# Rotating 96 images on one core: loads of 16 rows to a partition in place of 8

## The chip, the cores and the metric

One NeuronCore of one Trainium2 chip runs the kernel. The metric is device time in microseconds (us), the median of several runs. All runs quoted here are fast, that is, none was over 1.5% above the fastest of its kernel. The profile's span is some 1.8 us shorter than the device time, because it starts at the first instruction.

The traffic is 25.17 MB in and 25.17 MB out. "MB" of a slab or a buffer means 2^20 bytes; the profile's MB and GB/s are decimal. The profile also keeps a record of every packet (queue, start, duration, bytes); "by the records" below means that the bytes of each packet are spread over its duration, while the views count a packet whole where it starts.

## The reference

```python
def setup_inputs():
    batch, c, h, w = 32, 3, 256, 256
    return {"x": np.random.randn(batch, c, h, w).astype(np.float32)}

def reference(x):
    return np.rot90(x, k=-1, axes=(-2, -1)).astype(np.float32)
```

Each of the 96 images of 256 x 256 floats is rotated by 90 degrees clockwise: row h of the input becomes column 255 - h of the output.

## The kernel before

A slab is 1 MB, four images. Each partition gets 8 consecutive rows of an image (8 KB). VectorE transposes blocks of 32 partitions by 32 elements, after which each partition holds 8 consecutive output rows, and the slab is stored. Loads are issued from SyncE (SP in the profile), stores from ScalarE (ACT).

```python
    R = 8
    G = H // R
    n_slabs = B * C * G // P          # 24
    SHORT = 2
    ld_v = x.rearrange("b c h w -> (b c h) w").rearrange("(n p r) w -> n p (r w)", p=P, r=R)
    st_v = out.rearrange("b c h w -> (b c h) w").rearrange("(n p c) w -> n p (c w)", p=P, c=R)
    in_pool = ctx.enter_context(tc.tile_pool(name="in_pool", bufs=12))
    out_pool = ctx.enter_context(tc.tile_pool(name="out_pool", bufs=12))

    for n in range(n_slabs):
        t_in = in_pool.tile([P, R * W], fp32, tag="t_in")
        nc.sync.dma_start(out=t_in, in_=ld_v[n])
        t_out = out_pool.tile([P, R * W], fp32, tag="t_out")
        src = t_in.rearrange("p (r g c) -> p c r g", r=R, c=R)
        dst = t_out.rearrange("p (c g r) -> p c r g", c=R, r=R)[:, :, ::-1, ::-1]
        parts = 2 if n in (0, n_slabs - 1) else 1
        for k in range(parts):
            cs = slice(k * R // parts, (k + 1) * R // parts)
            nc.vector.transpose(out=dst[:, cs], in_=src[:, cs])
        nc.scalar.dma_start(out=st_v[n], in_=t_out,
                            max_dma_last_dim=2048 if n < SHORT else 8192)
    # (launch code cut)
```

`max_dma_last_dim` sets the size in bytes of one packet: the first two slabs are stored in 2 KB packets, the rest in 8 KB packets.

Of the kernel before, what the change touches and what calls it, by code (L numbers as in the profile page):

```python
# [1 line left out]

# [4 lines left out]


@with_exitstack  # L10
def kernel(
    ctx: ExitStack,
    tc: tile.TileContext,
    x: bass.AP,
    out: bass.AP,
):










    nc = tc.nc
    fp32 = mybir.dt.float32

    B, C, H, W = x.shape  # L30
    P = nc.NUM_PARTITIONS
    R = 8
    G = H // R
    n_slabs = B * C * G // P
    SHORT = 2

    ld_v = x.rearrange("b c h w -> (b c h) w").rearrange("(n p r) w -> n p (r w)", p=P, r=R)
    st_v = out.rearrange("b c h w -> (b c h) w").rearrange("(n p c) w -> n p (c w)", p=P, c=R)

    in_pool = ctx.enter_context(tc.tile_pool(name="in_pool", bufs=12))  # L40
    out_pool = ctx.enter_context(tc.tile_pool(name="out_pool", bufs=12))

    for n in range(n_slabs):
        t_in = in_pool.tile([P, R * W], fp32, tag="t_in")
        nc.sync.dma_start(out=t_in, in_=ld_v[n])  # L45

        t_out = out_pool.tile([P, R * W], fp32, tag="t_out")
        src = t_in.rearrange("p (r g c) -> p c r g", r=R, c=R)
        dst = t_out.rearrange("p (c g r) -> p c r g", c=R, r=R)[:, :, ::-1, ::-1]
        parts = 2 if n in (0, n_slabs - 1) else 1  # L50
        for k in range(parts):
            cs = slice(k * R // parts, (k + 1) * R // parts)
            nc.vector.transpose(out=dst[:, cs], in_=src[:, cs])  # L53

        nc.scalar.dma_start(out=st_v[n], in_=t_out,
                            max_dma_last_dim=2048 if n < SHORT else 8192)


# [1 line left out]
_INS = ['x']  # L60
_OUTS = [((32, 3, 256, 256), 'float32')]


# [23 lines left out]
```

## Time and profile before

| | before |
|---|---|
| device time, median of 3 (range) | 124.11 us (124.02 to 124.44) |
| span of the profile | 122.4 us |
| DMA: mean rate; plateau | 411 GB/s; about 428 GB/s |
| load queue, store queue: time of their packets | 49.1% and 49.0% of 16 engines' span |
| VectorE (DVE) busy | 91.6 us (75%) |

The page of the kernel before. The DVE and DMA rows show busy tenths in 40 equal slices of the span (9 is 90% or more), the GB/s row what moved in each slice; q1 is the load queue and q10 the store queue, with packets, MB and the time of their packets as a share of 16 engines' span.

```profile
span 122.4 us, 164 instructions
...
DVE  0199999999999999999999999697796793000000
...
DMA  2999999999999999999999999999999999999994
GB/s 83 426 428 428 390 428 424 422 421 426 424 428 418 428 426 420 426 428 428 426 428 428 428 428 428 428 426 426 428 428 428 426 428 428 428 428 426 428 428 193
...
q1 hardware_dynamic: 3456, 25.17, 49.1%
q10 hardware_dynamic: 4224, 25.17, 49.0%
```

The reader is to see that the DMA row is 9 in every slice but the first and the last, while VectorE stops being busy some 20 us before the end. Time can only be won by moving the same bytes at a higher rate, or by shortening the two ends. The one weak slice inside, 390 GB/s, is where the first stores join the loads.

### The profile page before, as it was taken

Reading aid. Unit: us, or ns where it says so; the run is one execution under the profiler, and the core shown is the slowest. Engines: PE = TensorE matmul, PEld = TensorE weight load, DVE = VectorE, ACT = ScalarE, POOL = GpSimd, SP = SyncE. Lnnn points to the kernel's source line nnn. Section 1 sums busy time; section 2 is a strip of 40 time slices with the busy share of each in tenths; the row PEclk is TensorE's granted clock in tenths of the full one; section 3 lists DMA queues with packets and bytes.
Section 4 is the critical chain, followed back from the end, with each engine's and each line's share of the span. In section 5 each row is a group of like instructions: output and inputs, shape, how many; then the busy total and the mean of one; then the engine's idle time right before and its main releaser. Section 6 shows DMA issues by size and latency. Waiting matters only on the chain.

```text
span 122.4 us, 164 instructions
## 1 busy us (share of the span) xinstructions
DVE 91.6 (75%) x26; POOL 0.2 (0%) x4
## 2 busy tenths in 40 slices
DVE  0199999999999999999999999697796793000000
POOL 0000000000000000000000000000000000000000
DMA  2999999999999999999999999999999999999994
GB/s 83 426 428 428 390 428 424 422 421 426 424 428 418 428 426 420 426 428 428 426 428 428 428 428 428 428 426 426 428 428 428 426 428 428 428 428 426 428 428 193
DMA packets 7680, 50.33 MB, mean 411 GB/s; under 512 B 768, under 2 KB 768, under 8 KB 1792
## 3 DMA queue, kind: packets, MB, share of 16 engines
q1 hardware_dynamic: 3456, 25.17, 49.1%
q10 hardware_dynamic: 4224, 25.17, 49.0%
HBM read 25.17 MB, written 25.17 MB: 411 GB/s over the span
## 4 chain that ended last, share of the span: by engine, by line
DMA 78%; DVE 2%; DVEq 2%; SPq 1%; issue 0%
DMA t_in<-in_x_dram 78%; DVE t_out L53 2%; DVEq L82 2%; SPq L45 1%; DVEq L53 0%
## 5 line engine op out<-in xcount | busy, mean ns | idle before, releaser
L53 DVE STREAM_TRANSPOSE t_out<-t_in 128x2048 f32<-128x2048 f32 (+1 forms) x26 | 91.6, 3647 | 10.4 <-DMA t_in<-in_x_dram 10.4
L71 POOL MEMSET const-bfloat16-1.0<- 128x1 bf16 x1 | 0.1, 102 | 0.0
L71 POOL MEMSET const-uint8-127<- 128x1 uint8 x1 | 0.1, 102 | 0.0
L71 POOL MEMSET const-float32-0.0<- 128x1 f32 x1 | 0.1, 99 | 0.2 <-issue 0.2
L71 POOL MEMSET const-float32-1.0<- 128x1 f32 x1 | 0.1, 99 | 0.0
## 6 DMA issues: line engine op xcount, KB each, us to landing
t_in<-in_x_dram SPq DMA_DIRECT2D x24, 1024.0 KB, 14.4
out_dram<-t_out ACTq DMA_DIRECT2D x24, 1024.0 KB, 19.5
```

The lines of the kernel that those rows point to most:

```text
L45: nc.sync.dma_start(out=t_in, in_=ld_v[n])
L53: nc.vector.transpose(out=dst[:, cs], in_=src[:, cs])
L71: nc = _bacc.Bacc("TRN2", target_bir_lowering=False, num_devices=1)
L82: with _tile.TileContext(nc) as tc:
```

## The change

Its intent: larger DMA packets. A slab becomes 2 MB (eight images); each partition gets 16 rows (16 KB) of one image. So that a block of 32 partitions still transposes into whole output partitions, the two halves of a slab are interleaved: two loads of 64 partitions each, one to the even and one to the odd partitions. The first slab keeps the old layout, so that work starts as soon as before, and is stored in 2 KB packets. Buffers halve in number and keep their bytes.

```diff
-    R = 8
-    SHORT = 2
+    RI, RO = 16, 8
+    K = H // RI
+    I = 2
+    Q = P // (K * I)
+    n_slabs = B * C // (Q * I)        # 12
...
-    in_pool = ctx.enter_context(tc.tile_pool(name="in_pool", bufs=12))
-    out_pool = ctx.enter_context(tc.tile_pool(name="out_pool", bufs=12))
+    in_pool = ctx.enter_context(tc.tile_pool(name="in_pool", bufs=6))
+    out_pool = ctx.enter_context(tc.tile_pool(name="out_pool", bufs=6))
     for n in range(n_slabs):
...
+        if n == 0:
+            for i in range(I):
+                nc.sync.dma_start(out=t_in[:, i], in_=ld8_v[n, i])
+                (transpose of half i, as before)
+        else:
+            t_flat = t_in.rearrange("p i f -> p (i f)")
+            for i in range(I):
+                nc.sync.dma_start(out=t_flat[i::I], in_=ld16_v[n, i])
+            src = t_flat.rearrange("p (r g c) -> p c r g", r=RI, c=RO)
+            dst = t_out.rearrange("p i (c k r) -> p c r k i", c=RO, r=RI)[:, :, ::-1, ::-1, :]
+            for h in range(2):
+                cs = slice(h * RO // 2, (h + 1) * RO // 2)
+                nc.vector.transpose(out=dst[:, cs], in_=src[:, cs])
+        for i in range(I):
+            nc.scalar.dma_start(out=st_v[n, i], in_=t_out[:, i],
+                                max_dma_last_dim=2048 if n == 0 else 8192)
```

More of the change, by code (lines that the diff above doesn't have):

```diff
@@ L31 @@
     P = nc.NUM_PARTITIONS
-    R = 8
-    G = H // R
-    n_slabs = B * C * G // P
-    SHORT = 2
-    ld_v = x.rearrange("b c h w -> (b c h) w").rearrange("(n p r) w -> n p (r w)", p=P, r=R)
-    st_v = out.rearrange("b c h w -> (b c h) w").rearrange("(n p c) w -> n p (c w)", p=P, c=R)
-    in_pool = ctx.enter_context(tc.tile_pool(name="in_pool", bufs=12))
-    out_pool = ctx.enter_context(tc.tile_pool(name="out_pool", bufs=12))
-    for n in range(n_slabs):
-        t_in = in_pool.tile([P, R * W], fp32, tag="t_in")
-        nc.sync.dma_start(out=t_in, in_=ld_v[n])
-        t_out = out_pool.tile([P, R * W], fp32, tag="t_out")
-        src = t_in.rearrange("p (r g c) -> p c r g", r=R, c=R)
-        dst = t_out.rearrange("p (c g r) -> p c r g", c=R, r=R)[:, :, ::-1, ::-1]
-        parts = 2 if n in (0, n_slabs - 1) else 1
-        for k in range(parts):
-            cs = slice(k * R // parts, (k + 1) * R // parts)
-            nc.vector.transpose(out=dst[:, cs], in_=src[:, cs])
-        nc.scalar.dma_start(out=st_v[n], in_=t_out,
-                            max_dma_last_dim=2048 if n < SHORT else 8192)
+    RI, RO = 16, 8
@@ new lines @@
+    K = H // RI
+    I = 2
+    Q = P // (K * I)
+    n_slabs = B * C // (Q * I)
+    rows_in = x.rearrange("b c h w -> (b c h) w")
+    rows_out = out.rearrange("b c h w -> (b c h) w")
+    ld8_v = rows_in.rearrange("(n i p r) w -> n i p (r w)", i=I, p=P, r=RO)
+    ld16_v = rows_in.rearrange("(n i m r) w -> n i m (r w)", i=I, m=Q * K, r=RI)
+    st_v = rows_out.rearrange("(n i p c) w -> n i p (c w)", i=I, p=P, c=RO)
+    in_pool = ctx.enter_context(tc.tile_pool(name="in_pool", bufs=6))
+    out_pool = ctx.enter_context(tc.tile_pool(name="out_pool", bufs=6))
@@ new lines @@
+    for n in range(n_slabs):
+        t_in = in_pool.tile([P, I, RO * W], fp32, tag="t_in")
+        t_out = out_pool.tile([P, I, RO * W], fp32, tag="t_out")
+        if n == 0:
+            for i in range(I):
+                nc.sync.dma_start(out=t_in[:, i], in_=ld8_v[n, i])
+                src = t_in[:, i].rearrange("p (r g c) -> p c r g", r=RO, c=RO)
+                dst = t_out[:, i].rearrange("p (c g r) -> p c r g", c=RO, r=RO)
+                nc.vector.transpose(out=dst[:, :, ::-1, ::-1], in_=src)
+        else:
[10 more added lines that the diff above has]
+                                max_dma_last_dim=2048 if n == 0 else 8192)
```

## The prediction

> **What bounds the kernel now.** The 16 DMA engines. In the sliced view the DMA row is 9 in all slices but the first and last, at about 428 GB/s; by windows, the DMA share is 1.01 from 3 to 98 us. The DMA queue table gives loads 49.1% and stores 49.0% of 16 engines' span: 120 us of packet time in a span of 122.4 us. VectorE is busy 91.6 us; from 78 us it waits for loads (about 0.95 us each), and its last transpose ends at 102 us, 20 us before the end: not the limit. After the last load packet (97 us) only stores run, still saturated.
>
> **What a packet costs.** The trace's packet records: 8192 bytes take 309 ns, 2048 bytes 84 ns. The line through both is 27.3 bytes/ns plus 9 ns per packet. The Trainium skill ("DMA: Bandwidth & Descriptors", Why small descriptors are slow) states a fixed overhead per packet; this trace agrees, with 9 ns.
>
> **What the change does.**
> - Removes: 22 of 24 MB of loads go in 16 KB packets, estimated at 609 ns instead of 2 x 309 = 618 ns. 1408 packets / 16 engines x 9 ns = 0.8 us, all on the critical path.
> - Unchanged: bytes, 24 loads, 24 stores, completions, 1024 store packets of 2 KB (two 1 MB slabs before, one 2 MB slab after). The first transpose still waits for one 1 MB load; the first store is still issued near 9.7 us.
> - Moves: queues alternate packet by packet (same page, Queues, rings and completion order, states round robin between queues; here 64 rounds of 309 + 84 ns are 25 us, and the 2 KB stores take about 23 us to drain). With 16 KB packets loads take two thirds, and 7/8 beside 2 KB stores: I estimate 64 x (609 + 84) = 44 us until slab 0 is stored, loads finished near 70 to 80 us instead of 97, and a longer pure store tail. That saves no bytes. VectorE will wait for output buffers rather than loads, and finish near 105 to 110 us; the final 2 MB of stores begin near 115 us, so some 7 us are spare.
> - VectorE: 24 transposes of 2048 elements (3.94 us each). The write's innermost step becomes 8 KB (two images), then 64 bytes backward, instead of 32 bytes. Both step to a new place each element; I expect 3.9 to 4.1 us. Up to about 4.5 us costs nothing; beyond it VectorE becomes the limit.
>
> **Prediction.** 124.1 - 0.8 = 123.3 us, plus 0.2 us for the coarser end: 123.5 us, 8 in 10 between 122.3 and 126.0. Faster by over 2%: 0.04; within: 0.82; slower: 0.14.
>
> **What would show it.** 1664 load data packets, 2048 with completions; the load queue's time down by 0.8 us; DMA row still 9 throughout, near 430 GB/s; transposes near 3.94 us; VectorE idle on stores of the output tile in the middle; loads finished well before 97 us.
>
> **What would make it wrong.** (1) The strided half-loads (every second partition) may spread badly over the SBUF's ports: 16 KB packets then take well over 620 ns and the rate falls below 428 GB/s: much slower. (2) The new write pattern slows the transpose past 4.5 us. (3) The starved stores fill the output buffers, VectorE stalls, and the end shows a hole in the DMA row. (4) Packets are cut smaller than 16 KB: no gain. No path that I see saves 2.5 us, as packets without any fixed cost would save only about 2.3 us.

## More of the kernel before

The kernel names no semaphores. The framework that it is written in deals them out, and puts in the waits.

The waits of SyncE's queue in the kernel before: who waited for what, us in total, number of times, longest.

```profile
SPq L45 <- DMA t_in<-in_x_dram: 68.4, 19, 4.6
SPq L82 <- DMA out_dram<-t_out: 42.7, 4, 35.5
...
SPq L45 <- DVE t_out L53: 0.3, 1, 0.3
```

Loads (L45) waited for earlier loads, and once for VectorE; none waited for a store. (L82 is the end of the kernel.)

## The result, and the profile after

| | before, same rounds | changed |
|---|---|---|
| device time, median of 6 (range) | 124.23 us (124.00 to 124.44) | 124.48 us (124.35 to 124.58) |
| ratio of the fast runs (95% interval) | | 1.002 (1.0004 to 1.0036) |
| ratio in a second comparison, five more rounds | | 0.9994 (0.9981 to 1.0008) |

A ratio is the mean time of one kernel's fast runs over that of the other's fast runs of the same rounds, so it is not quite the ratio of the medians. Within 0.2% either way the change did nothing: the 0.6 us that the prediction stood for did not appear. The time is inside the predicted range and in the likeliest of its three classes, which says little: the range was 3.7 us wide, six times the change that was forecast.

The page of the changed kernel:

```profile
span 122.6 us, 150 instructions
...
DVE  0199999993079999999999999999999997000000
...
DMA  3999999999999999999999999999999999999994
GB/s 94 428 446 433 433 402 297 394 433 460 396 457 414 428 428 430 444 412 436 428 430 422 438 433 433 438 409 438 433 428 412 428 428 428 428 428 428 428 428 195
...
q1 hardware_dynamic: 2048, 25.17, 49.2%
q10 hardware_dynamic: 4224, 25.17, 48.9%
```

Three things differ from before. The load queue has 2048 packets (1664 of data) in place of 3456, as predicted, yet its time is 49.2% of 122.6 us, no less than before. There is a hole in the GB/s row at the seventh slice (18.4 to 21.5 us), with 297 GB/s. The DMA row there still reads 9: packets were under way all the time, only they took longer. And VectorE, which should have been fed ahead of time, has a hole of its own a little later, near 30 us. (The slices of a profile with 16 KB packets scatter more than before, since a packet counts where it starts; a single slice of 460 says nothing.)

SyncE's waits in the changed kernel (L62 issues the 16 KB loads):

```profile
SPq L62 <- DMA t_in<-in_x_dram: 47.7, 14, 5.1
SPq L97 <- DMA out_dram<-t_out: 41.2, 4, 34.0
SPq L62 <- DMA out_dram<-t_out: 19.0, 2, 15.5
```

The third line is new: loads waited for stores, once for 15.5 us. (The other of the two, 3.4 us, is put down to a store but ended at 45.87 us, just as a load landed.) The start of the chain of waits (start, duration, what) shows which store the long wait was for:

```profile
0.73 4.79 DMA t_in<-in_x_dram
...
5.54 7.73 DVE t_out L58 x2
...
13.29 13.15 DMA out_dram<-t_out
...
26.46 0.47 SPq L62
```

The second store of the first slab was issued at 13.29 us and landed at 26.44 us, and only then was the eighth load issued. No data passes between them: the store writes the output of slab 0, and the load fills a fresh input buffer. The trace's records of the issues name the reason:

```
changed kernel                  before
load 7   issued 10.44 us        load 7   issued 10.61 us
load 8   waits semaphore 104    load 8   waits semaphore 104
         = store 2's                     = load 4's
load 8   issued 26.46 us        load 8   issued 13.11 us
```

A completion semaphore is a counter that tells that a DMA has landed. In these traces the DMAs of both queues use eight of them, dealt, as the order of their numbers shows, in the order in which the framework schedules the DMAs. A DMA that gets a semaphore anew is issued only when the last owner has landed. In the kernel before, loads and stores happened to alternate, so that every load took over from a load; of the stores two, the 4th and the 23rd, took over from a load, and neither waited long for it. In the changed kernel the first slab's two stores are scheduled one right after the other; the deal shifts by one, and load 8 gets the semaphore of a store of 512 packets of 2 KB that competes with the loads. When load 7 landed at 22.4 us the load queue was empty, and load 8 was issued only at 26.5 us.

The same stretches in both kernels by windows: us from and to, length, busy time and instructions of VectorE and of GpSimd, granted TensorE clock (not of use here), DMA share, GB/s. First the kernel before, then the changed one.

```profile
18.00:22.40 4.40, 4.40 (x2) 0.00 (x0) 1.00 1.02 424
22.40:26.00 3.60, 3.60 (x2) 0.00 (x0) 1.00 1.02 423
50.00:70.00 20.00, 20.00 (x7) 0.00 (x0) 1.00 1.01 426
```

```profile
18.00:22.40 4.40, 4.40 (x2) 0.00 (x0) 1.00 0.97 320
22.40:26.00 3.60, 3.60 (x2) 0.00 (x0) 1.00 1.07 421
50.00:70.00 20.00, 20.00 (x6) 0.00 (x0) 1.00 1.01 430
```

The steady stretch, 50 to 70 us, is faster, as the change intended, but by less than these lines suggest: by the records it is 427.5 GB/s before and 429.7 GB/s after, 0.5%. The loss is for the most part not where the load queue is empty (421 GB/s, 410 by the records) but in the 4 us before, while its last load is running out beside the 2 KB stores: 320 in place of 424 GB/s, or 341 in place of 423 by the records. In 4.4 us that is 82 / 423 x 4.4 = 0.85 us. The packet records show 16 KB packets of up to 1152 ns there, against 611 ns elsewhere.

The records give an account. For a moment in the kernel before, ask when the changed kernel had moved as many bytes. At 18 us it is 0.29 us ahead; at 26 us it is 0.67 us behind; from 98 us to the end it is 0.22 us behind, which is the difference of the spans. So 0.96 us are lost from 18 to 26 us, and 0.74 us are won elsewhere: 0.29 us before that, when the first stores join (0.1 us of it in the first 4 us, which may be chance), and 0.45 us after it. (In the repeat of the changed kernel below: 0.26 us ahead, 0.69 us behind, 0.26 us behind.)

### The profile page after: what moved, and what is told of

The parts are those of the page before. It is cut to its first block, busy times and chain, and to the rows that moved or that the text cites. A ratio compares the mean times of both kernels' runs of the same rounds, so it can differ in the third digit from the quotient of the medians.

```text
span 122.6 us, 150 instructions
## 1 busy us (share of the span) xinstructions
DVE 92.1 (75%) x24; POOL 0.2 (0%) x4
## 3 DMA queue, kind: packets, MB, share of 16 engines
q1 hardware_dynamic: 2048, 25.17, 49.2%
## 4 chain that ended last, share of the span: by engine, by line
DMA 63%; DVE 16%; DVEq 4%; SPq 1%; issue 0%
DMA t_in<-in_x_dram 52%; DMA out_dram<-t_out 11%; DVE t_out L67 9%; DVE t_out L58 6%; DVEq L97 4%; SPq L62 1%; DVEq L67 0%
## 5 line engine op out<-in xcount | busy, mean ns | idle before, releaser
L67 DVE STREAM_TRANSPOSE t_out<-t_in 128x2048 f32<-128x2048 f32 x22 | 84.6, 3989 | 5.8 <-DMA t_in<-in_x_dram 5.8
L58 DVE STREAM_TRANSPOSE t_out<-t_in 128x2048 f32<-128x2048 f32 x2 | 7.7, 3938 | 5.5 <-DMA t_in<-in_x_dram 5.5
```

The lines of the kernel that those rows point to most:

```text
L58: nc.vector.transpose(out=dst[:, :, ::-1, ::-1], in_=src)
```

## The experiments

The theory (A): the larger packets do save about half a microsecond, and it is given back because load 8 waits for a store and the load queue runs out beside 2 KB stores. Rival B: a 16 KB packet beside 2 KB stores is slow in itself, with or without the semaphore. Rival C: 16 KB packets save nothing.

### The eighth load with its own semaphore (e1_own_sem)

The loads of slab n+1 are written before the stores of slab n, and the second store is scheduled after the fourth load, an edge that costs no wait. The built program then gives load 8 the semaphore of load 4 and, in exchange, store 6 that of store 2. By the trace, all other semaphores and the order of each queue are as in the changed kernel. (Store 6 was issued at 50.9 us, when store 2 had landed; its queue had other stores to run until 71.9 us.)

```diff
+    loads = []
+    def load(n):   (the two loads of slab n; each appended to loads)
...
+        if n + 1 < n_slabs:
+            t_next = load(n + 1)
         for i in range(I):
-            nc.scalar.dma_start(...)
+            s = nc.scalar.dma_start(...)
+            if n == 0 and i == 1:
+                tc.add_manual_dep(s.ins, loads[3].ins.name, mybir.DependencyInfo(
+                    mybir.DependencyClass.NoSync, mybir.DependencyReason.DATA), reason="order")
```

> The changed kernel with one difference: the eighth load no longer shares its completion semaphore with the second store, but with the fourth load, as in the kernel before. Theory A (16 KB packets save about 0.6 us of packet time; it is given back because the eighth load waits for the second store until 26.4 us, the load queue runs dry, and 18 to 22.4 us run at under 300 GB/s): no dry load queue, at least 415 GB/s from 18 to 23 us, 123.5 us, ratio to before 0.994. Rival B (a 16 KB packet beside 2 KB stores is slow in itself): the slow stretch stays or is longer, 124.3 us or more. Rival C (16 KB packets save nothing): the slow stretch may go, but the steady stretch from 36 to 78 us is no faster than before; 124.0 us or more.

Measured: 123.85 us, ratio to before 0.9952 (0.9938 to 0.9967). Its page, SyncE's waits, and the windows of the stretch that was slow:

```profile
span 121.8 us, 150 instructions
...
GB/s 97 425 436 430 452 410 405 453 432 404 444 432 405 447 440 399 416 425 412 430 438 436 430 417 417 417 430 430 430 425 428 430 428 428 430 428 428 428 428 207
...
q1 hardware_dynamic: 2048, 25.17, 49.0%
```

```profile
SPq L111 <- DMA out_dram<-t_out: 59.6, 4, 52.4
SPq L58 <- DMA t_in<-in_x_dram: 48.2, 19, 4.5
```

```profile
18.00:22.40 4.40, 4.40 (x2) 0.00 (x0) 1.00 1.02 429
22.40:26.00 3.60, 3.60 (x2) 0.00 (x0) 1.00 0.99 419
```

Loads (L58) wait for loads alone, the hole is gone, and the kernel beats both of the others. Rival B falls: here 16 KB loads ran beside 2 KB stores until 50 us at full rate. This run also behaves as the prediction described the changed kernel: slab 0 stored at 50 us, loads finished at 75.7 us, and VectorE waiting for output buffers (10.1 us). None of the three was so in the changed kernel.

One thing that I had named as a sign of rival C did turn up: from 36 to 78 us this kernel was no faster than the one before (426 against 427 GB/s). But that stretch holds a slow one of its own, at 50 to 52 us, where the stores change from 2 KB to 8 KB packets (376 GB/s by the records; 0.18 us are lost there by the account of the records). From 55 to 75 us, clear of such changes, the records give 429.7 GB/s here against 427.5 before.

Repeated with the changed kernel in the same rounds:

> The changed kernel again, on the same chip and in the same rounds as the next run, to compare the two directly: ratio to before 1.001 to 1.003.

> The changed kernel with the eighth load's own semaphore again: ratio to before 0.994 to 0.997, so 0.6 to 0.9 us under the changed kernel. If the difference seen so far was one between chips or rounds, the two come out within 0.2 us.

Measured: the changed kernel 124.29 us, ratio 0.9994 (0.9981 to 1.0008); with its own semaphore 123.74 us, ratio 0.9955 (0.9943 to 0.9968). So the shared semaphore costs (0.9994 - 0.9955) x 124.3 = 0.5 us in these rounds, somewhat less than the (1.002 - 0.9952) x 124.3 = 0.85 us of the first comparisons; the changed kernel came out 0.3% better than the first time, outside what I expected of it. The intervals of the two kernels do not overlap, so the difference is not one between chips or rounds. The profile of the repeat again has the hole (324 GB/s from 18 to 22.4 us), and that of the other again does not (438). The whole times differ by less than the 0.96 us lost from 18 to 26 us, in part because of the slow stretch at 50 to 52 us, which only the kernel with its own semaphore has.

### The same with 8 KB load packets (e2_own_sem_8k_loads)

```diff
-                d = nc.sync.dma_start(out=t_in.rearrange(...)[i::I], in_=ld16_v[n, i])
+                d = nc.sync.dma_start(out=t_in.rearrange(...)[i::I], in_=ld16_v[n, i],
+                                      max_dma_last_dim=8192)
```

> The same as the run before it, but the loads cut into 8 KB packets (same bytes, tiles and order). Theory A: the packet saving is undone, 124.1 to 124.2 us, 0.6 us over the run before it. Rival B: faster than the run before it, as 16 KB packets are the slow ones. Rival C: equal to the run before it within 0.1 us.

Measured: 124.17 us, ratio 0.9989 (0.9974 to 1.0004), so 0.0037 x 124.4 = 0.46 us over the run before it. Not all of the 0.46 us is the cost of packets: the GB/s row also has two weak slices, 378 and 404, near 34 to 40 us, where the stores change from 2 KB to 8 KB packets.

```profile
GB/s 85 427 427 427 404 418 422 435 427 412 417 378 404 427 430 427 430 427 427 430 427 427 427 427 430 427 430 427 427 427 427 427 427 427 427 427 427 427 427 197
```

By the account of the records this execution (the slowest of the five) loses 0.47 us there against the kernel before, and e1 0.18 us at its own change. What settles rival C is the steady rate. By the records, from 55 to 75 us, the four kernels with 8 KB loads and 8 KB stores (before, e2, e3, e8) all run at 427.5 GB/s, and all executions with 16 KB loads at 429.3 to 429.7. A 16 KB load and an 8 KB store, 24 KB on one of 16 engines, so take 915.3 ns in place of 919.8: 4.5 ns for the packet spared, 0.4 us for the 88 spared on each engine. So rival C falls, and the rest of what e1 gains lies at the start and where the mix of the queues changes.

### The kernel before, with the semaphore shared (e3_before_shared_sem)

```diff
+        if n == 3:   (load 4 scheduled after store 2)
+            tc.add_manual_dep(d.ins, stores[1].ins.name, ...NoSync...)
+        if n == 4:   (store 3 scheduled after load 5, as in the changed kernel)
+            tc.add_manual_dep(stores[2].ins, d.ins.name, ...NoSync...)
```

> The kernel before, with the eighth load made to share the second store's completion semaphore, as the changed kernel has it. Theory A, if the dry load queue alone is what costs: loads stop near 22 us until near 26 us, and the time rises by about 0.9 us to 125.1 us. Rival B (16 KB packets are needed for the loss): loads stop all the same, but the rate stays above 410 GB/s and the time within 0.2 us of before.

Measured: 124.90 us, ratio 1.0048 (1.0024 to 1.0072): 0.6 us lost, two thirds of what was expected, and with 8 KB loads, so that larger packets are not needed for the loss. SyncE's wait, the windows, and the page's GB/s row:

```profile
SPq L46 <- DMA out_dram<-t_out: 15.4, 1, 15.4
```

```profile
18.00:22.40 4.40, 4.40 (x2) 0.00 (x0) 1.00 1.02 378
22.40:26.00 3.60, 3.60 (x2) 0.00 (x0) 1.00 1.08 423
```

```profile
GB/s 85 424 432 427 393 419 378 387 437 427 427 427 429 432 427 427 427 427 427 427 427 429 427 432 427 427 432 427 429 429 427 427 429 427 427 427 427 427 384 216
```

Again a wait of 15.4 us, and again most of the loss lies before the queue is empty, not after: in the records the slow load packets (median 482 ns, against 309) stand between 20.5 and 22 us. By the account of the records, this execution is 0.56 us behind at 26 us. It loses 0.4 us more near the end (the slice of 384): the loads lasted until 113.6 us in place of 97.6, VectorE's last transpose ended at 118.2 us, and the last stores had to wait for it. So the 0.6 us are the cost of the edit as a whole, and the load queue that ran out is not all of it. The changed kernel has no such second loss.

### The queue run dry for another reason (e7_own_sem_3_bufs)

```diff
 (on e1_own_sem)
-    in_pool = ctx.enter_context(tc.tile_pool(name="in_pool", bufs=6))
+    in_pool = ctx.enter_context(tc.tile_pool(name="in_pool", bufs=3))
```

> The changed kernel with its own semaphore, but 3 input buffers in place of 6, so that the load queue runs dry for another reason (loads wait for VectorE) while the 2 KB stores still run. If a load queue running dry beside 2 KB stores is what loses rate: one or more stretches under 350 GB/s of 2 to 3 us before 30 us, and about 0.8 us more than the run with the semaphore alone changed, 124.6 us or more. If it is the semaphore wait and nothing else: no such stretch, within 0.2 us of 123.85 us.

Measured: 124.11 us, ratio 0.9986 (0.9971 to 1.0000), 0.0034 x 124.3 = 0.4 us more than e1. The page's GB/s row:

```profile
GB/s 80 428 439 428 450 413 422 287 455 436 425 404 423 447 428 428 434 412 428 442 428 437 415 436 442 426 442 404 426 428 428 428 423 423 426 426 428 428 428 217
```

One slice falls to 287 GB/s (21.4 to 24.5 us), where the load queue runs out for the first time because loads now wait for VectorE to free a buffer. The semaphore is not needed for the loss. The size was half of what I expected. Later the queue ran out again, near 32 us, and lost little (410 GB/s in the worst microsecond of the records, with load packets of the usual 611 ns), so a queue that runs out beside 2 KB stores doesn't lose rate every time.

### First stores in 8 KB and in 4 KB packets (e4, e6, e8, e9)

If a load queue running out loses rate beside 2 KB stores only, 8 KB first stores should mend the changed kernel. The edit in e4 is on the changed kernel, in e6 and e9 on e1, in e8 on the kernel before (there as `SHORT = 0`, to the same effect):

```diff
-   max_dma_last_dim=2048 if n == 0 else 8192
+   max_dma_last_dim=8192                          (e9: 4096 if n == 0 else 8192)
```

> The changed kernel with the first slab stored in 8 KB packets instead of 2 KB; the shared semaphore stays. Theory A (a dry load queue loses rate only because 2 KB stores are what is left to run): the second store lands sooner or as soon, no stretch under 400 GB/s, 123.2 to 123.4 us. If the dry queue loses rate whatever the stores' packet, 124.0 us or more. Rival C: 124.0 us or more.

> The changed kernel with its own semaphore for the eighth load and the first slab stored in 8 KB packets. If what the 8 KB first stores cost in the run with the shared semaphore was a stretch of slow loads as the first stores join (11.3 to 14.7 us, 375 GB/s), it is here too, and the time is 0.3 to 0.5 us above the run with only the semaphore changed: 124.2 us, ratio 0.998. If the 8 KB first stores cost nothing in themselves, the fewer packets show: 123.6 us, ratio 0.993.

> The kernel before with all stores in 8 KB packets. If joining 8 KB stores slow the loads by themselves (as in the changed kernel with 8 KB first stores, where about 0.6 us went): a stretch under 400 GB/s around 12 to 15 us, and 124.3 to 124.7 us, no gain from 768 packets fewer. If not: 768 / 16 x 4.6 = 0.2 us faster than before, no slow stretch.

> Own semaphore, first slab stored in 4 KB packets, between the 2 KB and 8 KB of the earlier runs. If the slow loads at the join grow with the size of the joining packets: a shortfall at 10 to 15 us between 0.02 us (2 KB) and 0.56 us (8 KB), and one near the change to 8 KB packets under the 0.2 us of 2 KB; in sum 123.7 us, equal within 0.15 us to both neighbours, ratio 0.995. If the size does not matter there: a shortfall of 0 or of 0.5 us.

| run | on | first stores | us | ratio to before (95%) | GB/s, 11 to 15 us |
|---|---|---|---|---|---|
| e4 | changed | 8 KB | 124.27 | 0.9978 (0.9956 to 0.9999) | 358 |
| e6 | e1 | 8 KB | 123.72 | 0.9955 (0.9942 to 0.9968) | 369 |
| e8 | before | 8 KB | 124.29 | 1.0002 (0.9990 to 1.0013) | 340 |
| e9 | e1 | 4 KB | 123.70 | 0.9951 (0.9938 to 0.9963) | 415 |
| e1 | changed | 2 KB | 123.85 | 0.9952 (0.9938 to 0.9967) | 411 |
| before | | 2 KB | | 1 | 400 |

SyncE's wait in e4, and the window in which its load queue runs out:

```profile
SPq L62 <- DMA out_dram<-t_out: 15.1, 1, 15.1
```

```profile
22.40:26.00 3.60, 3.60 (x2) 0.00 (x0) 1.00 0.99 419
```

In e4 the load queue ran out at 24 us because of the same wait (15.1 us), and the rate held at about 427 GB/s in the records there. So this running out, beside 8 KB stores, cost nothing; beside 2 KB stores it cost in the changed kernel, its repeat, e3 and the first time in e7, and not the second time there. But e4 missed its 123.2 to 123.4 us: a slow stretch appeared elsewhere, at 11 to 15 us, where 8 KB stores join the loads (and a shorter one from 32 to 33.5 us, where they join again after their queue was empty). The first is in all three kernels with 8 KB first stores, whatever the loads' packets and the semaphores, and it eats the packets saved. It shows what the 2 KB packets of the first slab are good for. My figure for e6 (0.998) was too gloomy: it has that stretch and lacks another, when e1's stores change from 2 KB to 8 KB packets at 50 to 52 us (about 375 GB/s in e1's records), so the two tie. With 4 KB both stretches are mild, and the time is the same again, as expected. A few tenths of a microsecond are left in these joins, and none of the three settings gets at them.

### The cost of a packet by itself (e5_before_4k_stores)

```diff
 (on the kernel before)
-                            max_dma_last_dim=2048 if n < SHORT else 8192)
+                            max_dma_last_dim=2048 if n < SHORT else 4096)
```

> The kernel before with its 22 large stores cut into 4 KB packets: 2816 more packets, same bytes. It measures the cost of a packet by itself. As predicted blind (9 ns per packet): 2816 / 16 x 9 = 1.6 us more, ratio 1.013. As the rates of the traces suggest now (2 KB alone run at 409 GB/s, so one in 80.1 ns on each engine, 8 KB alone at 427.5 GB/s, one in 306.6 ns; the line through both leaves 4.6 ns per packet): 0.8 us more, ratio 1.0065. Rival C (packet size costs nothing): ratio 1.000.

Measured: 124.80 us, ratio 1.0042 (1.0029 to 1.0055): 0.0042 x 124.3 = 0.52 us for 2816 / 16 = 176 more packets on each engine, 3.0 ns each (2.1 to 3.9 by the interval), below both of my figures and clear of rival C's zero. The durations of the records alone would say 9 ns: a 4 KB packet has 159 ns there, one of 8 KB 309 ns. But the records of one engine overlap a little, hence the shares above 1.00 in the DMA column of the windows. Where stores run alone, first the kernel before, then this one:

```profile
105.00:118.00 13.00, 0.00 (x0) 0.00 (x0) 1.00 1.01 429
```

```profile
105.00:118.00 13.00, 0.00 (x0) 0.00 (x0) 1.00 1.03 421
```

By the records these are 427.5 and 421.1 GB/s, so 8 KB on one of 16 engines take 306.6 ns and twice 4 KB take 311.3 ns: 4.7 ns for the added packet.

## Why the prediction was right or wrong

- **What bounds the kernel**: right. DMA binds in every run here (but for a microsecond at the end of e3), and VectorE finished at 103.5 us in the changed kernel without costing anything.
- **"1408 packets / 16 engines x 9 ns = 0.8 us, all on the critical path"**: this step failed, in its size. The 9 ns was read from durations of records that overlap. The added packet costs 3 ns end to end in the doubling experiment, 4.7 ns where stores run alone, and the spared one saves 4.5 ns in the steady stretch. For 88 packets on each engine that is 0.3 to 0.4 us, half of the 0.8 us.
- **"Unchanged: bytes, 24 loads, 24 stores, completions" and "DMA row still 9 throughout, near 430 GB/s"**: this is the step that turned the gain into nothing. The row stayed 9, the rate did not stay near 430: 0.96 us were lost from 18 to 26 us. The prediction listed what the change leaves as it was and counted the 24 loads among it. It never asked which completion semaphore each load would get. In the changed kernel the eighth load waited 15.5 us for a store; undoing that gives 0.9952 and 0.9955, and doing that to the kernel before costs 0.6 us, at least half of it in the same place. The wait is part of the program, as the trace's record of the issue shows, so a listing of the built program's waits should show it before any run; I did not look.
- **"loads finished near 70 to 80 us", "44 us until slab 0 is stored", VectorE waiting for output buffers**: wrong of the changed kernel (94.6 us; stored at 26.1 us; VectorE waited 5.8 us for loads instead), right of the kernel with its own semaphore (75.7 us; slab 0 stored at 50 us after joining at 13 us, so 37 us; 10.1 us on stores). The mechanism of the queues taking turns packet by packet was right in the main: from 20 to 45 us that kernel ran 568 load packets and 693 store packets, so somewhat more than one store to a load, and 37 us in place of 44.
- **VectorE, 3.9 to 4.1 us for a transpose**: right, 3989 ns on average against 3936 ns.
- **The risks**: the interleaved half loads did not spread badly (611 ns packets, 429 GB/s from 8.5 to 12.5 us with loads alone), packets were not cut, and there was no hole at the end.
- **That no path saves 2.5 us**: right; the best versions here save 0.6 us (0.0049 x 124.3).

Still open is why load packets stretch, most of them to 1.2 to 1.8 times their usual duration, for 1 to 4 us in three situations: a load queue running out beside 2 KB stores, 8 KB stores joining, and stores changing from 2 KB to 8 KB packets. No run here measures the reason.

## What to carry to other kernels

Before counting what a change saves on a saturated queue, list which instruction every DMA's issue will wait for. A framework that deals a few completion semaphores to all DMAs can make a load wait for an unrelated store, and a shift by one in the order of scheduling is enough. And measure the cost of a packet by adding packets and timing the whole: durations of overlapping records overstate it (9 ns against 3.0 to 4.7 ns here).

## What the Trainium skill lacked or had wrong

- "DMA: Bandwidth & Descriptors", section "Why a DMA increments its semaphore by 16 and not by 1", advises one semaphore per slot in flight, so that no wait passes before its data has landed. It lacks what sharing costs in time when loads and stores draw from the same eight: a wait of 15.5 us here, and 0.5 to 0.85 us of the total.
- The same page, section "Queues, rings and completion order", says that an engine drains a packet, typically of some 9 to 17 descriptors, before it turns to the next queue. With packets of 2 KB and more, the turns here were for the most part one record to one: between 20 and 25 us of the kernel before, 203 loads of 8 KB and 221 stores of 2 KB. Equal numbers alone would also fit longer turns, but the record that starts 2 to 5 ns before a load's end, a gap that stands out in the records as that between one packet and the next on an engine, is a store in nearly nine cases of ten (chance coincidences taken off).
- The same page, section "Why small descriptors are slow (HBM only)", gives a fixed overhead for each packet, and calls putting consecutive descriptors into one packet worth it at 256 bytes and less. The section has no measurement at larger sizes. Here the overhead is still measurable at 4 KB: 0.52 us in 124.3 us for 2816 packets more, 3.0 ns per packet on each engine.
- The same page, "Rules for kernel authors", advises against two transfers to disjoint halves of the partitions, as both share the same 16 engines. It does not say that nothing need be lost by it: two transfers of every second partition, 64 to a transfer, ran at full rate, 429 GB/s with these loads alone (8.5 to 12.5 us of the changed kernel's records). No page has a measurement of every second partition; those of "SBUF — State Buffer" are of neighbouring ones.
- No page has the slow stretches at a change in the mix of the queues: 340 to 370 GB/s from 11 to 15 us when 8 KB stores join, 320 GB/s over 4.4 us (341 by the records) when a load queue runs out beside 2 KB stores.
